# Two of the four slices of the experts' second product computed as split products

## The chip, the cores and the metric

One core of a Trainium2 chip runs the kernel. The metric is the device time of one execution in microseconds (us), as the median of several runs.

## The reference

One layer of a generator: a mixer (a recurrent part and an attention part, both on 1024 latent tokens behind 256 context tokens), and then a mixture of 32 experts, of which each token takes four. Only the experts matter here. For an expert with the tokens `xblk` gathered for it:

```python
u = xblk @ w1[e] + b1[e]                       # 1024 -> 2048
glu = jnp.minimum(u[:, 0::2], SWIGLU_LIMIT)
lin = jnp.clip(u[:, 1::2], -SWIGLU_LIMIT, SWIGLU_LIMIT)
return (glu * jax.nn.sigmoid(SWIGLU_ALPHA * glu) * (lin + 1.0)) @ w2[e] + b2[e]   # 1024 -> 1024
```

The rows are then scaled by the gates and added to the token stream, and a norm ends the layer. Everything is in float32.

## The kernel before

The mixer's instructions are put in order by a planner (class Weave), whose helper at line 954 issues them, so that they all carry that line. The last part of it routes the tokens, loads the first slices of the first expert and converts them (Route.loads, line 684, Route.conversions, line 698).

Then come 32 jobs, one for each expert, in a fixed order that lets sizes alternate (`TURN`, line 100). A job has N places for tokens: by `NS`, line 99, 13 jobs have 128, four 132, nine 136 to 156, three 160, and one each 168, 192 and 200. Experts.run (line 452) issues all instructions in the order written there, with no planner: each job has twelve steps, s = 0 to 11, one for each weight slice of 1 MB (128 x 2048 float32). Slices 0 to 7 belong to the first product, 8 to 11 to the second.

A slice of the first product is computed as a **split product**. ScalarE copies the slice into a rounded form, fp32r (hi, line 342, the instruction is at line 348); VectorE subtracts that from the slice and leaves the rest in bf16 (lo, line 351, at line 356). The tokens lie in both forms too, side by side (tokens, line 316: transposes at 326, ScalarE's copy at 328, VectorE's subtraction at 329). In products (line 371) 16 matmuls of the rounded weights go over both halves of the tokens, 2N columns (line 382), and 16 of the bf16 rests over the tokens' upper halves, N columns (line 386). sums (line 402) adds the two column halves of the result: ScalarE reads the second with the bias (407), VectorE adds the first (408) and clips (409, 410); gate (414) and hidden (417) follow.

A slice of the second product is computed **unsplit**, in plain float32 with N columns (line 393, 32 matmul instructions in the trace); ScalarE scales the result into yT (scaled, line 419, at 423). The first of them, s = 8, reads the hidden values of slices 6 and 7 last (`late`, line 390).

The tables `HI` and `LO` (lines 160, 161) say in which step which split slice, counted over the jobs, is converted:

```python
W1, W2 = 4, 4
HI = {0: 4, 1: 5, 2: 6, 3: 7, 5: 8, 7: 9, 8: 10, 9: 11}
LO = {s + 1: c for s, c in HI.items()}
```

So ScalarE converts four to two steps ahead of need, and VectorE one step after ScalarE. Converted slices have four places (ring "wc"), raw ones of the first product four (ring "w1") and of the second four (ring "w2"). lo asks SP for the load four split slices ahead (load1, line 362); run asks for the unsplit slices of the next job right after each unsplit product (load2, line 367), where SP waits until TensorE has read the place. SP's queue is in order.

Beside the slices, step 0 of a job computes the next job's slots (slots, line 283: matmuls at 292 on the one-hots, then eight small VectorE operations for each block of 128 tokens), step 1 starts its gather on GpSimd, step 8 transposes its tokens, and steps 8 to 11 make one-hots for the job after that, two in each step (onehots, line 275, at 281). Steps 1 to 4 transpose the job before's output rows (438, 439), and GpSimd scatters them (444). Results of the products go to two places of two PSUM banks in turn (ring "pe"); the slots' and transposes' go to four others.

Of the kernel before, what the change touches and what calls it, by code (L numbers as in the profile page):

```python
# [157 lines left out]

W1, W2 = 4, 4
HI = {0: 4, 1: 5, 2: 6, 3: 7, 5: 8, 7: 9, 8: 10, 9: 11}  # L160
LO = {s + 1: c for s, c in HI.items()}

# [17 lines left out]
class Experts:  # L180
# [23 lines left out]
    def place(self, sets):  # L204
# [16 lines left out]
        lo = HL  # L221
        for tag, n, width, dt in (("HH", 1, 8 * most, F32), ("u", 2, 2 * most, F32), ("sg", 2, most, F32)):
            self.ring(tag, cols(lo, n, width, dt))
            lo += n * width
        mid = lo
        assert lo + 2048 <= ROOM
        self.ring("yo", cols(sb + 3072, 3, D))
        self.ring("yT", cols(spare, 1, 8 * most))
        self.ring("wc", [(at(c, 2048, dt=F32R), at(c + 2048, 1024, dt=BF)) for c in (end, sa, sa + 3072, sb)])
        self.ring("w1", cols(sc, 3, 2048) + [at(low, 2048)])  # L230
        self.ring("w2", cols(end + 3072, 2, 2048) + [at(spare + 8 * most, 2048), at(mid, 2048)])
        lo = tt
# [99 lines left out]
    def load(self, J, s):  # L332
        nc = self.nc
        if s == 0:
            bi = self.t("bi", 24)
            nc.sync.dma_start(bi, self.a["bexp"][bass.ds(J["e"], 1)].rearrange("o p n -> p (o n)"))
            J["bi"] = bi
        w = self.t("w1" if s < 8 else "w2", 2048)
        nc.sync.dma_start(w, self.a["wexp"][bass.ds(J["e"], 1), s].rearrange("o p n -> p (o n)"))
        J["w", s] = w  # L340

    def hi(self, n):

        J, s = self.first(n)
        if J:
# [5 lines left out]
    def lo(self, n):  # L351

        J, s = self.first(n)
        if J:
# [3 lines left out]

    def first(self, n):
        return (self.jobs[n // 8], n % 8) if n < 8 * len(self.jobs) else (None, 0)  # L360

    def load1(self, n):
        J, s = self.first(n)
        if J:
            self.load(J, s)

    def load2(self, n):
        if n < 4 * len(self.jobs):
            self.load(self.jobs[n // 4], 8 + n % 4)

    def products(self, J, s):
# [3 lines left out]
        J["p", s] = p  # L375
        if s < 8:
            X = J["X"]
            xt = X.rearrange("p k s n -> p (k s n)").bitcast(BF).rearrange("p (k s n t) -> p k s n t", k=KT, s=2, t=2)
# [37 lines left out]
    def hidden(self, J, s):  # L416
        self.nc.vector.tensor_mul(J["H"][:, s], J.pop(("u", s))[:, 1], J.pop(("sg", s)))  # L417

    def scaled(self, J, s):
        nc, N, p = self.nc, J["N"], J.pop(("p", s))  # L420
        for q in range(2):
            c = 2 * s - 16 + q
            nc.scalar.activation(J["yT"][:, c], p[:, q, :N], AF.Identity, bias=J["b2"][:, 8 + c:9 + c],  # L423
                                 scale=self.gt2[:, c:c + 1])

# [26 lines left out]
    def run(self, fast=True, beside=None):  # L452
# [4 lines left out]
        for i in range(12 * len(jobs)):  # L457
# [4 lines left out]
            if s == 0:  # L462
                self.biases(J)
                J["H"] = self.t("HH", KT, J["N"])
                J["yT"] = self.t("yT", KT, J["N"])
# [9 lines left out]
            else:  # L475
                self.scaled(J, s)
                self.load2(4 * j + s - 4)
            if s in HI:
                self.hi(8 * j + HI[s])
            if s < 7:  # L480
                self.gate(J, s)
            if s in LO:
                self.lo(8 * j + LO[s])
            if s == 8 and nxt:
# [112 lines left out]
    def block(self, i):  # L597
# [19 lines left out]
        for s in range(4):  # L617
            self.hi(s)
            self.lo(s)
        self.run(False)  # L620
# [13 lines left out]
class Route:  # L634
# [49 lines left out]
    def loads(self):  # L684
        w, ex = self.w, self.ex
        yield self.placed
        yield self.rwkv.end
        for n, s in enumerate((0, 1, 2, 8, 9, 3, 10, 11)):
            if n == 3:
# [8 lines left out]
    def conversions(self):  # L698
        w, ex = self.w, self.ex
        for s in range(4):  # L700
# [3 lines left out]
            ex.hi(s)  # L704
            yield self.loaded[3]
            yield "dve"
# [2205 lines left out]
```

## Time and profile before

| | |
|---|---|
| median of 3 runs | 2736.94 us (2735.51 to 2742.81) |
| the profiled execution | 2734.6 us |
| its span, first to last instruction | 2732.8 us |
| TensorE busy | 2548.0 us, 93% of the span |
| VectorE, ScalarE busy | 1889.3 us (69%), 1461.1 us (53%) |
| first split product of the experts | 1267.86 us from the span's start |

In the rows PE is TensorE's matmuls, PEld its weight loads, DVE VectorE, ACT ScalarE, POOL GpSimd and SP the engine that issues most DMAs. Lengths of operations overlap on an engine; what an operation costs its engine is read from one start to the next. The idle time in square brackets is that ahead of the operation, with what ended it.

### The profile page before, as it was taken

Reading aid. Unit: us, or ns where it says so; the run is one execution under the profiler, and the core shown is the slowest. Engines: PE = TensorE matmul, PEld = TensorE weight load, DVE = VectorE, ACT = ScalarE, POOL = GpSimd, SP = SyncE. Lnnn points to the kernel's source line nnn. Section 1 sums busy time; section 2 is a strip of 40 time slices with the busy share of each in tenths; the row PEclk is TensorE's granted clock in tenths of the full one; section 3 lists DMA queues with packets and bytes.
Section 4 is the critical chain, followed back from the end, with each engine's and each line's share of the span. In section 5 each row is a group of like instructions: output and inputs, shape, how many; then the busy total and the mean of one; then the engine's idle time right before and its main releaser. Section 6 shows DMA issues by size and latency. Waiting matters only on the chain.

```text
span 2732.8 us, 58537 instructions
## 1 busy us (share of the span) xinstructions
PE 2548.0 (93%) x23428; PEld 2240.4 (82%) x23428; DVE 1889.3 (69%) x3925; ACT 1461.1 (53%) x2489; POOL 508.0 (19%) x455
## 2 busy tenths in 40 slices
PE   6999886989999997986999999999999999999996
PEld 3667664678677786665999999999999999999995
DVE  7745888867776638677676675766667676766765
ACT  6323333546544533234665665766656666666664
POOL 1112564411111136210011100110101010011101
PEclk8999987879999988997999999999999999999998
DMA  6741324253243145665887896988888988889884
GB/s 259 260 150 56 110 91 161 101 150 94 87 122 106 52 145 157 234 205 203 296 326 261 312 334 252 321 323 301 324 317 309 334 295 324 308 321 323 306 334 147
DMA packets 212183, 622.50 MB, mean 228 GB/s; under 512 B 49400, under 2 KB 127352, under 8 KB 160576
## 3 DMA queue, kind: packets, MB, share of 16 engines
q1 hardware_dynamic: 201008, 581.95, 59.1%
q0 software_dynamic: 10896, 36.74, 5.5%
q8 instruction: 186, 3.05, 0.4%
q14 instruction: 93, 0.76, 0.1%
HBM read 544.09 MB, written 74.53 MB: 226 GB/s over the span
## 4 chain that ended last, share of the span: by engine, by line
PE 72%; DVE 18%; DMA 3%; issue 3%; ACT 3%; POOL 1%; SPq 1%; DVEq 0%; ACTq 0%; POOLq 0%
PE banks L954 24%; PE banks L382 18%; PE banks L393 18%; DVE at L954 14%; PE banks L386 9%; ACT at L954 2%; DVE at L356 2%; PE banks L438 2%; PE banks L326 1%; POOL at L954 1%; DVE at L408 1%; SPq L954 1%; PE banks L292 0%; DVE at L409 0%; DMA at<-vh_d 0%
## 5 line engine op out<-in xcount | busy, mean ns | idle before, releaser
L954 PE MATMUL banks<-at,at 128*128 128x512 f32 (+10 forms) x3810 | 753.4, 355 | 54.4 <-POOL at L954 18.9
L954 PEld LDWEIGHTS banks<-at,at 128*128 128x128 f32 (+3 forms) x3290 | 451.4, 188 | 209.7 <-issue 82.3
L356 DVE TENSOR_TENSOR at<-at,at 128x2048 bf16<-128x2048 f32 x252 | 576.2, 2287 | 54.8 <-ACT at L348 53.9
L382 PE MATMUL banks<-at,at 128*128 128x256 f32 (+11 forms) x4096 | 601.8, 300 | 0.0
L382 PEld LDWEIGHTS banks<-at,at 128*128 128x128 f32 x4096 | 548.7, 190 | 1.2
L393 PE MATMUL banks<-at,at 128*128 128x128 f32 (+11 forms) x4096 | 521.5, 287 | 6.6 <-DVE at L417 6.0
L393 PEld LDWEIGHTS banks<-at,at 128*128 128x128 f32 x4096 | 505.0, 191 | 13.7 <-DVE at L417 12.9
L348 ACT ACTIVATE at<-at 128x2048 fp32r<-128x2048 f32 x252 | 481.5, 1911 | 0.0
L954 ACT ACTIVATE at<-banks 128x512 f32<-128x512 f32 (+6 forms) x475 | 239.6, 525 | 362.3 <-PE banks L954 339.5
L408 DVE TENSOR_TENSOR at<-banks,at 128x256 f32<-128x256 f32 (+11 forms) x256 | 115.6, 452 | 316.3 <-ACT at L407 304.3
L954 DVE TENSOR_TENSOR at<-at,at 128x1024 fp32r<-128x1024 f32 (+26 forms) x388 | 281.3, 736 | 57.0 <-ACT at L954 38.6
L407 ACT ACTIVATE at<-banks,at 128x128 f32<-128x128 f32 (+11 forms) x512 | 189.3, 380 | 226.1 <-PE banks L386 186.8
L386 PE MATMUL banks<-at,at 128*128 128x128 bf16 (+11 forms) x4096 | 306.0, 226 | 0.0
L954 ACT ACTIVATE at<-at 128x512 f32<-128x512 f32 (+10 forms) x259 | 175.9, 701 | 202.6 <-DVE at L954 108.3
L386 PEld LDWEIGHTS <-at 128*128 128x128 bf16 x4096 | 258.1, 96 | 17.6 <-issue 3.0
L954 PE MATMUL banks<-at 128*64 128x64 f32 (+4 forms) x4880 | 231.7, 232 | 36.8 <-DMA at<-w_d 18.6
L954 PEld LDWEIGHTS banks<-at 128*64 128x64 f32 (+3 forms) x4880 | 204.8, 143 | 68.7 <-issue 18.6
L954 POOL TENSOR_TENSOR at<-at,at 64x512 f32<-64x512 f32 (+5 forms) x130 | 185.9, 1439 | 308.0 <-DVE at L954 279.5
L423 ACT ACTIVATE at<-banks,at,modc 128x128 f32<-128x128 f32 (+11 forms) x256 | 116.9, 469 | 203.7 <-PE banks L393 203.5
L954 PE MATMUL banks<-kc,at 128*128 128x128 f32 (+4 forms) x1136 | 182.7, 291 | 44.5 <-ACT at L954 17.2
L312 POOL DMA_INDIRECT at<-h_d,at x49 | 47.5, 969 | 892.0 <-DVE at L294 364.1
L954 POOL TENSOR_TENSOR at<-at 128x512 f32<-128x512 f32 (+3 forms) x94 | 129.8, 1387 | 431.2 <-PE banks L954 132.3
(155 smaller groups left out, 2015.6 us busy)
## 6 DMA issues: line engine op xcount, KB each, us to landing
at<-in_wexp SPq DMA_DIRECT2D x384, 1024.0 KB
at<-in_mod_w SPq DMA_DIRECT2D x48, 512.0 KB
at<-w_d SPq DMA_DIRECT2D x48, 384.0 KB
w_d<-at SPq DMA_DIRECT2D x16, 1024.0 KB
at<-w_d SPq DMA_DIRECT2D x32, 512.0 KB
at<-in_w_in SPq DMA_DIRECT2D x18, 512.0 KB
x_d<-at SPq DMA_DIRECT2D x18, 512.0 KB
at<-in_x SPq DMA_DIRECT2D x16, 512.0 KB
```

Of the source, the lines that this page charges most:

```text
L312: nc.gpsimd.indirect_dma_start(out=xg[:R], out_offset=None, in_=self.d["h2"], in_offset=bass.IndirectOffsetOnAxis(ap=gi[:R, 0:1], axis=0))
L326: nc.tensor.transpose(p[:, k, :R], xg[:R, kk * 128:kk * 128 + 128], ident[:R, :R])
L348: self.nc.scalar.activation(wh, J["w", s], AF.Copy)
L356: self.nc.vector.tensor_sub(wl, J.pop(("w", s)), wh.bitcast(F32))
L382: nc.tensor.matmul(p[:, q, :2 * N], wh[:, k, q], X[:, k].rearrange("p s n -> p (s n)"), start=k == 0, stop=False, skip_group_check=True)
L386: nc.tensor.matmul(p[:, q, N:2 * N], wl[:, k, q], xt[:, k, 0, :, 1], start=False, stop=k == KT - 1, skip_group_check=True)
L393: nc.tensor.matmul(p[:, q, :N], w[:, k, q], J["H"][:, k], start=k == 0, stop=k == KT - 1, skip_group_check=True)
L407: nc.scalar.activation(u[:, q], p[:, q, N:2 * N], AF.Identity, bias=b)
L408: nc.vector.tensor_add(u, p[:, :, :N], u)
L423: nc.scalar.activation(J["yT"][:, c], p[:, q, :N], AF.Identity, bias=J["b2"][:, 8 + c:9 + c], scale=self.gt2[:, c:c + 1])
L438: nc.tensor.transpose(p[:R, k * 128:k * 128 + 128], J["yT"][:, 4 * j + k, b0:b0 + R], self.K("ident"))
L954: return f(*args, **kw)
```

## The change

Slices 10 and 11, the last two of the second product, become split products as well (`SPLIT`). So a job has ten split slices, which are counted and converted in the same rows of `HI` and `LO`, now with ten entries each; a conversion on VectorE that belongs to step 11's copy falls into step 0 of the next job (`LO[0] = 3`, thirteen slices on). The hidden values get two forms after step 7 (halves): ScalarE copies them into fp32r, VectorE subtracts, each in one instruction over all 8 x N columns. Slices 8 and 9 still read the plain values. In scaled the split slices take ScalarE's scaled reading of the second column half, and VectorE adds the first with the same scale (scalar_tensor_tensor). Raw slices of the split kind get five places, the unsplit ones two; the hidden values move to a place of their own. Before the first job seven slices are loaded by Route.loads instead of eight, and lo waits there for slice 4.

```diff
--- before.py
+++ after.py
@@ -156,9 +156,10 @@
     return o
 
 
-W1, W2 = 4, 4
-HI = {0: 4, 1: 5, 2: 6, 3: 7, 5: 8, 7: 9, 8: 10, 9: 11}
-LO = {s + 1: c for s, c in HI.items()}
+W1, W2 = 5, 2
+SPLIT = (0, 1, 2, 3, 4, 5, 6, 7, 10, 11)
+HI = {0: 4, 1: 5, 2: 6, 3: 7, 5: 8, 7: 9, 8: 10, 9: 11, 10: 12, 11: 13}
+LO = {0: 3, 1: 4, 2: 5, 3: 6, 4: 7, 6: 8, 8: 9, 9: 10, 10: 11, 11: 12}
 
 
 def inverse_root(e, y, x, t):
@@ -219,16 +220,16 @@
         self.tables, low = lo, HL - 2048
         assert lo + 400 <= low
         lo = HL
-        for tag, n, width, dt in (("HH", 1, 8 * most, F32), ("u", 2, 2 * most, F32), ("sg", 2, most, F32)):
+        for tag, n, width, dt in (("HH", 1, 16 * most, F32R), ("u", 2, 2 * most, F32), ("sg", 2, most, F32)):
             self.ring(tag, cols(lo, n, width, dt))
             lo += n * width
-        mid = lo
-        assert lo + 2048 <= ROOM
+        assert lo <= ROOM
         self.ring("yo", cols(sb + 3072, 3, D))
         self.ring("yT", cols(spare, 1, 8 * most))
         self.ring("wc", [(at(c, 2048, dt=F32R), at(c + 2048, 1024, dt=BF)) for c in (end, sa, sa + 3072, sb)])
-        self.ring("w1", cols(sc, 3, 2048) + [at(low, 2048)])
-        self.ring("w2", cols(end + 3072, 2, 2048) + [at(spare + 8 * most, 2048), at(mid, 2048)])
+        self.ring("w1", cols(sc, 3, 2048) + [at(low, 2048), at(spare + 8 * most, 2048)])
+        self.ring("w2", cols(end + 3072, 2, 2048))
+        self.ring("H", cols(spare + 8 * most + 2048, 1, 8 * most))
         lo = tt
 
         def one(n, dt=F32):
@@ -335,13 +336,13 @@
             bi = self.t("bi", 24)
             nc.sync.dma_start(bi, self.a["bexp"][bass.ds(J["e"], 1)].rearrange("o p n -> p (o n)"))
             J["bi"] = bi
-        w = self.t("w1" if s < 8 else "w2", 2048)
+        w = self.t("w1" if s in SPLIT else "w2", 2048)
         nc.sync.dma_start(w, self.a["wexp"][bass.ds(J["e"], 1), s].rearrange("o p n -> p (o n)"))
         J["w", s] = w
 
     def hi(self, n):
 
-        J, s = self.first(n)
+        J, s = self.split(n)
         if J:
             wh, wl = self.rings["wc"][0]
             self.rings["wc"].append(self.rings["wc"].pop(0))
@@ -350,31 +351,32 @@
 
     def lo(self, n):
 
-        J, s = self.first(n)
+        J, s = self.split(n)
         if J:
             wh, wl = J["c", s]
             self.nc.vector.tensor_sub(wl, J.pop(("w", s)), wh.bitcast(F32))
             self.load1(n + W1)
 
-    def first(self, n):
-        return (self.jobs[n // 8], n % 8) if n < 8 * len(self.jobs) else (None, 0)
+    def split(self, n):
+        j, i = divmod(n, len(SPLIT))
+        return (self.jobs[j] if j < len(self.jobs) else None), SPLIT[i]
 
     def load1(self, n):
-        J, s = self.first(n)
+        J, s = self.split(n)
         if J:
             self.load(J, s)
 
     def load2(self, n):
-        if n < 4 * len(self.jobs):
-            self.load(self.jobs[n // 4], 8 + n % 4)
+        if n < 2 * len(self.jobs):
+            self.load(self.jobs[n // 2], 8 + n % 2)
 
     def products(self, J, s):
         nc, N = self.nc, J["N"]
         p = self.rings["pe"][0]
         self.rings["pe"].reverse()
         J["p", s] = p
-        if s < 8:
-            X = J["X"]
+        if s in SPLIT:
+            X = J["X"] if s < 8 else J["HH"]
             xt = X.rearrange("p k s n -> p (k s n)").bitcast(BF).rearrange("p (k s n t) -> p k s n t", k=KT, s=2, t=2)
             wh, wl = (x.rearrange("p (k s c) -> p k s c", k=KT, s=2) for x in J.pop(("c", s)))
             for q in range(2):
@@ -416,12 +418,24 @@
     def hidden(self, J, s):
         self.nc.vector.tensor_mul(J["H"][:, s], J.pop(("u", s))[:, 1], J.pop(("sg", s)))
 
+    def halves(self, J):
+
+        HH = J["HH"] = self.t("HH", KT, 2, J["N"])
+        self.nc.scalar.activation(HH[:, :, 0], J["H"], AF.Copy)
+        self.nc.vector.tensor_sub(HH[:, :, 1], J["H"], HH[:, :, 0].bitcast(F32))
+
     def scaled(self, J, s):
         nc, N, p = self.nc, J["N"], J.pop(("p", s))
         for q in range(2):
             c = 2 * s - 16 + q
-            nc.scalar.activation(J["yT"][:, c], p[:, q, :N], AF.Identity, bias=J["b2"][:, 8 + c:9 + c],
-                                 scale=self.gt2[:, c:c + 1])
+            u = J["u2"] = self.t("u", 2, N) if s in SPLIT and q == 0 else J.get("u2")
+            nc.scalar.activation(u[:, q] if s in SPLIT else J["yT"][:, c], p[:, q, N:2 * N] if s in SPLIT else p[:, q, :N],
+                                 AF.Identity, bias=J["b2"][:, 8 + c:9 + c], scale=self.gt2[:, c:c + 1])
+        if s in SPLIT:
+            for q in range(2):
+                c = 2 * s - 16 + q
+                nc.vector.scalar_tensor_tensor(J["yT"][:, c], p[:, q, :N], self.gt2[:, c:c + 1], u[:, q],
+                                               op0=OP.mult, op1=OP.add)
 
     def rows(self, J, i):
 
@@ -461,7 +475,7 @@
             far = jobs[j + 2] if j + 2 < len(jobs) else None
             if s == 0:
                 self.biases(J)
-                J["H"] = self.t("HH", KT, J["N"])
+                J["H"] = self.t("H", KT, J["N"])
                 J["yT"] = self.t("yT", KT, J["N"])
             self.products(J, s)
             if s < 8:
@@ -474,13 +488,16 @@
                     self.hidden(J, s)
             else:
                 self.scaled(J, s)
-                self.load2(4 * j + s - 4)
+                if s not in SPLIT:
+                    self.load2(2 * j + s - 6)
             if s in HI:
-                self.hi(8 * j + HI[s])
+                self.hi(len(SPLIT) * j + HI[s])
             if s < 7:
                 self.gate(J, s)
-            if s in LO:
-                self.lo(8 * j + LO[s])
+            if s in LO and (i or not fast):
+                self.lo(len(SPLIT) * j + LO[s])
+            if s == 7:
+                self.halves(J)
             if s == 8 and nxt:
                 self.tokens(nxt)
             if j == 0 and nxt and s == 1:
@@ -616,7 +633,8 @@
         self.tokens(J)
         for s in range(4):
             self.hi(s)
-            self.lo(s)
+            if s < 3:
+                self.lo(s)
         self.run(False)
 
     def final(self, out):
@@ -685,7 +703,7 @@
         w, ex = self.w, self.ex
         yield self.placed
         yield self.rwkv.end
-        for n, s in enumerate((0, 1, 2, 8, 9, 3, 10, 11)):
+        for n, s in enumerate((0, 1, 2, 8, 9, 3, 4)):
             if n == 3:
                 yield self.outputs
             if n == 5:
@@ -702,7 +720,7 @@
             yield self.loaded[s]
             yield "act"
             ex.hi(s)
-            yield self.loaded[3]
+            yield self.loaded[4]
             yield "dve"
             ex.lo(s)
```

## Rows read from the trace of the kernel before

**Rows 1.** The page, part 4: the chain that ended last, by line
```profile
PE banks L954 24%; PE banks L382 18%; PE banks L393 18%; DVE at L954 14%; PE banks L386 9%; ACT at L954 2%; DVE at L356 2%; PE banks L438 2%; PE banks L326 1%; POOL at L954 1%; DVE at L408 1%; SPq L954 1%; PE banks L292 0%; DVE at L409 0%; DMA at<-vh_d 0%
```

**Rows 2.** Windows: span, busy PE PEld DVE ACT POOL, granted clock, DMA share, GB/s
```profile
1300.00:2680.00 1380.00, 1373.53 (x13104) 1344.16 (x13104) 946.92 (x2063) 886.16 (x1441) 142.19 (x97) 1.00 0.86 309
2222.37:2264.10 41.73, 41.37 (x435) 40.52 (x434) 30.41 (x71) 28.37 (x48) 7.31 (x4) 1.00 0.92 330
```

**Rows 3.** Timeline of TensorE, end of a 128-token job: start, us, line, form
```profile
2238.97 2.08 PE L382 MATMUL banks<-at,at 128*128 128x256 f32 x16
...
2247.55 1.55 PE L393 MATMUL banks<-at,at 128*128 128x128 f32 x12
2249.47 2.50 PE L393 MATMUL banks<-at,at 128*128 128x128 f32 x20 [0.36 <-DVE at L417]
...
2253.36 10.98 PE L393 MATMUL banks<-at,at 128*128 128x128 f32 x96
2264.10 2.43 PE L382 MATMUL banks<-at,at 128*128 128x296 f32 x16
```

**Rows 4.** Timeline of TensorE, the 148-token job behind it
```profile
2284.96 2.43 PE L382 MATMUL banks<-at,at 128*128 128x296 f32 x16
...
2288.26 2.42 PE L382 MATMUL banks<-at,at 128*128 128x296 f32 x16
...
2296.86 12.25 PE L393 MATMUL banks<-at,at 128*128 128x148 f32 x96
2308.85 2.16 PE L382 MATMUL banks<-at,at 128*128 128x256 f32 x16
```

**Rows 5.** Timeline of VectorE, one step of the 128-token job
```profile
2230.39 0.42 DVE L408 TENSOR_TENSOR at<-banks,at 128x256 f32<-128x256 f32 x1 [1.38 <-issue]
2230.85 0.23 DVE L409 TENSOR_SCALAR at<-at 128x128 f32<-128x128 f32 x1
2230.99 0.22 DVE L410 TENSOR_SCALAR at<-at 128x128 f32<-128x128 f32 x1
2231.13 0.28 DVE L417 TENSOR_TENSOR at<-at,at 128x128 f32<-128x128 f32 x1
2231.33 2.28 DVE L356 TENSOR_TENSOR at<-at,at 128x2048 bf16<-128x2048 f32 x1
2233.53 0.42 DVE L408 TENSOR_TENSOR at<-banks,at 128x256 f32<-128x256 f32 x1
```

**Rows 6.** Groups by line and form: busy us, mean ns, idle before
```profile
L348 ACT ACTIVATE at<-at 128x2048 fp32r<-128x2048 f32 x252 | 481.5, 1911 | 0.0
...
L954 ACT ACTIVATE at<-at 128x1024 fp32r<-128x1024 f32 x42 | 44.1, 1054 | 58.3 <-PE banks L954 31.3 <-DVE at L954 10.7 <-DMA at<-in_w_in 6.5
L954 DVE TENSOR_TENSOR at<-at,at 128x1024 fp32r<-128x1024 f32 x34 | 43.4, 1284 | 27.1 <-ACT at L954 17.1 <-PE banks L954 9.5 <-issue 0.2
...
L329 DVE TENSOR_TENSOR at<-banks,at 128x80 fp32r<-128x80 f32 x2 | 0.4, 231 | 0.0
...
L408 DVE TENSOR_TENSOR at<-banks,at 128x256 f32<-128x256 f32 x104 | 43.8, 421 | 118.5 <-ACT at L407 109.4 <-issue 8.9
...
L954 DVE SCALAR_TENSOR_TENSOR at<-banks,kc,at 128x512 f32<-128x512 f32 x10 | 7.4, 745 | 0.1
```

**Rows 7.** Timeline of VectorE around the turn of a job
```profile
2161.67 2.29 DVE L356 TENSOR_TENSOR at<-at,at 128x2048 bf16<-128x2048 f32 x1 [1.51 <-ACT at L348]
...
2212.96 0.42 DVE L281 TENSOR_SCALAR at<-at,at 128x148 bf16<-128x148 bf16 x2
...
2225.91 0.42 DVE L408 TENSOR_TENSOR at<-banks,at 128x256 f32<-128x256 f32 x1 [6.49 <-ACT at L407]
```

**Rows 8.** Waits of SP's queue: us in total, times, longest us
```profile
SPq L339 <- PE banks L393: 324.0, 124, 5.2
```

**Rows 9.** Windows, as in rows 2, before the first expert
```profile
1260.00:1265.00 5.00, 2.94 (x16) 2.20 (x14) 3.07 (x10) 3.28 (x5) 0.00 (x0) 0.50 0.02 5
```

**Rows 10.** Groups by line: the slot matmuls
```profile
L292 PE MATMUL banks<-at,at 128*128 128x8 bf16 x248 | 11.6, 167 | 3.1 <-DVE at L281 3.1
```

## The prediction

> **What bounds the kernel now.** I read the page's chain first: TensorE holds most of it, and behind the helper line of the mixer (24%) its pieces are lines 382 and 386 (split products, 18% and 9%) and 393 (unsplit ones, 18%) [rows 1]. Only the expert stage is changed, so I cut it out by windows: from 1300 to 2680 us TensorE is busy for 1373.5 of 1380 us at the granted clock 1.00, with VectorE at 947, ScalarE at 886 and the DMA share at 0.86 [rows 2]. So a job (one expert) costs what its matmuls cost. The only regular gap of TensorE there is at the first unsplit slice, 0.36 us in a job of 128 tokens [rows 3].
>
> **Term 1, matmuls removed: -46 us.** Prices are start-to-start times of whole slices. With 128 tokens three unsplit slices run from 2253.36 to 2264.10, 3.58 us each; three split ones from 2238.97 to 2247.55, 2.86 us each [rows 3]: 0.72 us saved per slice. With 148 tokens it is (2308.85 - 2296.86)/3 = 4.00 against 3.30, 0.70 saved [rows 4]. 26 of the 32 jobs have 128 to 156 tokens, six have 160 to 200 and hardly save less: 64 slices x 0.72 = 46 us. That is the ceiling: the rest of TensorE's work is the same.
>
> **Term 2, what VectorE must do more.** In a 128-token job of 41.73 us it is busy for 30.4 us [rows 2]. Added are two conversions (2.28 us long, but the next operation starts 2.20 us after: 2231.33 to 2233.53 [rows 5]), one subtraction of 128x1024 into fp32r (1.28 us), and four scalar_tensor_tensor of 128x128 out of PSUM [rows 6]. The last has no row of its own: above the 0.23 us of 128x80 and below the 0.42 us of 128x256, both plain sums out of PSUM; a scalar_tensor_tensor of 128x512 takes 0.75, on the line that these two make (0.23 + 432 x 0.0011 = 0.70) but for 0.05 [rows 6]. I take 0.33, midway. Together 4.4 + 1.3 + 1.3 = 7.0, so 37.4 us of work. The job's matmuls will need 41.73 - 2 x 0.72 = 40.3 us. That fits, but VectorE works in order, and I followed the order step by step:
>
> - Step 7: the subtraction of the second half stands behind ScalarE's copy (1.05 us [rows 6]), and that behind a conversion of 1.9 us. Before, VectorE already waited 1.51 us there for that conversion [rows 7]; now it waits about 2.5, then subtracts. Behind it stand the conversion of step 8, the subtractions of the next tokens and the one-hots. They move back by 2.2 us, and TensorE doesn't feel it there: slices 8 and 9 take the values as they were, and slice 10, the first reader of the halves, begins 9.4 us after slice 7's end (5.81 to the end of slice 8's transposes, 2247.55 to 2253.36, and 3.58 [rows 3]), the halves being ready after some 6.
> - Steps 8 to 11: 2.20 of conversion in each, 0.35 of one-hots in each (0.42 for two, end included [rows 7]), and 0.7 of scalar_tensor_tensor in steps 10 and 11. VectorE's idling ahead of each new job, 6.49 us here [rows 7], is used up.
> - The turn of the job. Slice 11 ends at time E. ScalarE's second read ends near E + 0.6, the second scalar_tensor_tensor near E + 0.9, the conversion that now stands in step 11 near E + 3.1, the two one-hots near E + 3.5. Ahead of them step 10 may still be at work, up to 0.3 more. TensorE has its slot matmuls (line 292), which read those one-hots, right behind slice 0: at E + 2.86 with 128 tokens, E + 3.30 with 148. **A new wait of TensorE on line 281**, 0.3 to 0.9 us in all but the largest jobs. I take 0.7 in 30 jobs: +21 us, bounds 9 and 27.
> - Steps 0 to 4: in step 0 a conversion is added ahead of the slots' small operations; then each step is 3.14 us (2230.39 to 2233.53 [rows 5]) against TensorE's 2.86 and a few transposes in a small job. Nothing is caught up until step 5, which has none. The hidden product of slice 6, for which the first unsplit slice waits, comes 0.1 to 0.8 later: 17 small jobs x 0.2 = +3 us, bounds 2 and 14.
>
> **What costs nothing.** ScalarE gets two conversions (1.91 each) and a copy: 28.4 + 4.9 of 41 us in a small job [rows 2, 6]; that is hidden under TensorE, and only the copy's place, priced above, matters. The loads are as many. 64 of the 128 that waited for TensorE's unsplit slices (324 us of SP's standing [rows 8]) now follow a conversion; chunk n + 5 is asked for when chunk n is converted, four or five steps ahead, 13 us or more, against 3.4 us for each slice in the stream (41 us over 12). Behind SP's wait stand only later loads and the small gate and bias reads. Before the first job lo() waits for one load more, but the DMA engines stand at 0.02 from 1260 to 1265, so it has landed [rows 9]. PSUM of slices 10 and 11 comes free 0.3 us later, still a slice ahead of need. The end gains two scalar_tensor_tensor ahead of the last transposes: +0.7 us.
>
> **The sum.** -46 + 21 + 3 + 1 = -21 us. The profiled execution took 2734.6 us (span 2732.8), 2.3 below the median of the three runs, so 2713.6 in its terms and about 2716 for a median of new runs.
>
> **A rule against the change.** The chain of [rows 5] shows that operations of VectorE overlap: the conversion is followed 0.08 us before its end, and five operations whose lengths add to 3.43 us take 3.14. The Trainium skill, VectorE: DVE Perf Modes, section "The DRAIN you can't avoid", says that the next operation does not start until the pipe is empty, and allows an earlier start only for one that is not held; the trace agrees with that exception. By the rule alone a small job would ask 37.4 + 4.2 (the overlaps of 71 operations) + 2.5 = 44.1 us of VectorE, 2.4 more than it takes now, and 17 of them would make the kernel some 40 us slower instead of 21 faster.
>
> **Rivals.** (a) VectorE is never late enough to hold TensorE: the idling at the turn was large, and TensorE waited 3.1 us in all for one-hots so far [rows 10]. Against it: the order above. It would give the ceiling, 2734.6 - 46, some 2690 as a median. Chance 0.12. (b) VectorE sets the pace. Place: the closed loop from its step 7 round to the next, with the wait of 2.5 us in it. In a small job it has 37.4 + 2.5 = 39.9 against 40.3. There each microsecond beyond what I priced is paid at some 25 of the 31 turns (the largest jobs have room): 0.85 us more a job and the gain is gone, 2 us more and it is -21 + 50 = 29 us slower, 2766. Operations that don't overlap would do it: 71 a job x 0.06 is 4 us. For it: the thin margin, four unmeasured operations, the waits between ScalarE and VectorE. Against: in steps 1 to 4 of today's small jobs VectorE already runs without a gap at 3.14 a step, and TensorE doesn't wait [rows 3, 5]. Chance slower 0.15, about even 0.17. (c) Loads hold the products: the small job's window moves 330 GB/s at a share of 0.92 [rows 2]; 1.7% less time asks for 0.94. A slice would have to take over 3.5 us in the stream. It would eat some 10 us: 2726. Chance 0.04.
>
> **How the numbers follow.** My case (TensorE still the bound, less one wait at each turn) has 0.52, with its own range, from the bounds of the terms (-46 + 9 + 2 + 1 = -34 and -46 + 27 + 14 + 1 = -4), from 2703 to 2733. About 0.3% (8 us) is what a measurement of this kernel can tell from no change. Faster: 0.52 + 0.12 + 0.04 = 0.68; same 0.17; slower 0.15. The range goes from the ceiling nearly reached, 2692 (waits of 2 us in all), to 2741, which takes in the even case of (b) and leaves out its slow one and a little of (a).
>
> **What would show it.** Right: line 393 with half its instructions, line 382 and 386 a quarter more; jobs of 128 tokens near 41 us; VectorE busy about 37 us of that; "DVE at L281" as the releaser of line 292's matmuls, some 20 us in 30 times; VectorE's gap ahead of a job gone; the wait on line 417 a little above 0.36 in a small job. Wrong: line 382 held by the conversions (line 356) or by the sums (line 408) in most small jobs, which is (b); line 356's conversions on ScalarE waiting for loads, which is (c); or TensorE at 99.5% as before, which is (a).

## The result, and the profile after

The changed kernel takes 2705.4 us (median of four runs, 2704.5 to 2719.4) against 2736.4 for the kernel before (2735.5 to 2742.8): a ratio of 0.9894, interval 0.9858 to 0.9929, 31 us less by the medians. The profiled execution took 2705.2 us, its span 2703.4. Forecast: 2716, range 2692 to 2741.

The same views as before, now with the line numbers of the changed kernel: split products at 384 and 388, unsplit ones at 395, slot matmuls at 293 on the one-hots of 282, VectorE's conversions at 357, sums at 409 (ScalarE) and 410, biases at 401 and 402, hidden values at 419, the halves at 424 and 425, scalar_tensor_tensor at 437. First the chain, which answers to [rows 1].

```profile
PE banks L972 24%; PE banks L384 15%; DVE at L972 15%; DVE at L357 9%; PE banks L395 8%; PE banks L388 7%; ACT at L972 2%; DVE at L410 2%; PE banks L327 1%; DVE at L411 1%; SPq L972 1%; ACT at L409 1%; ACT at L349 1%; DVE at L412 1%; PE banks L452 1%
```

The unsplit products fell from 18% to 8%. New in the chain is VectorE's conversion, 9% where it had 2%: VectorE now takes part in setting the pace of the experts. The windows (columns as in [rows 2]), the expert stage and one job of 128 tokens:

```profile
1300.00:2650.00 1350.00, 1333.56 (x13084) 1296.06 (x13084) 1153.89 (x2281) 1027.00 (x1532) 166.75 (x97) 1.00 0.90 315
2200.09:2241.18 41.09, 40.20 (x436) 39.12 (x434) 36.50 (x77) 32.74 (x52) 7.52 (x4) 1.00 0.93 324
```

That is the same job as in [rows 2]: 41.09 us instead of 41.73, VectorE busy for 36.5 instead of 30.4. TensorE's two gaps are in its timeline, the turn and the first unsplit slice, and, from the job behind it (148 tokens), the next turn:

```profile
2200.09 2.13 PE L384 MATMUL banks<-at,at 128*128 128x256 f32 x16
...
2203.00 0.29 PE L293 MATMUL banks<-at,at 128*128 128x8 bf16 x6
2203.67 0.63 PE L293 MATMUL banks<-at,at 128*128 128x8 bf16 x10 [0.38 <-DVE at L282]
2204.23 2.16 PE L384 MATMUL banks<-at,at 128*128 128x256 f32 x16
...
2227.97 2.50 PE L395 MATMUL banks<-at,at 128*128 128x128 f32 x20 [0.51 <-DVE at L419]
...
2244.51 0.66 PE L293 MATMUL banks<-at,at 128*128 128x8 bf16 x8
2245.02 2.42 PE L384 MATMUL banks<-at,at 128*128 128x296 f32 x16
```

Before the change the slot matmuls took 0.55 us from the first to the next slice in this job, now 1.23 (2203.00 to 2204.23): 0.68 lost, of which the row labels 0.38 as waiting. So I measure from start to start. I cut each of 29 jobs (the second to the thirtieth) at its first slot matmul, at slice 1, at the first unsplit slice, at the token transposes and at the unsplit slice behind them, and summed the differences from the kernel before:

| us over 29 jobs | slot matmuls | slices 1 to 7 | first unsplit slice | the rest | all |
|---|---|---|---|---|---|
| the change | +13.7 | +0.5 | +3.0 | -42.4 | -25.1 |

Each number is rounded by itself, and all come from one profiled execution of each kernel. The mixer's end also moved, 1267.86 to 1263.80 for the first split product. That is not the change's: in the changed kernel and its variants below the same mixer ends between 1252.7 and 1275.4, and the mixer of the kernel before at 1267.86 in one profile and at 1277.56 in another (e10). So the experiments are read by both: the 29 jobs from the timelines, and the ratio of the times.

Three groups by line, which answer to [rows 10] and, for the loads, to [rows 8], and the waits of SP's queue:

```profile
L293 PE MATMUL banks<-at,at 128*128 128x8 bf16 (+11 forms) x392 | 24.0, 169 | 10.1 <-DVE at L282 9.9
L395 PE MATMUL banks<-at,at 128*128 128x128 f32 (+11 forms) x2048 | 271.5, 289 | 11.8 <-DVE at L419 11.4
L349 ACT ACTIVATE at<-at 128x2048 fp32r<-128x2048 f32 x316 | 603.3, 1909 | 0.0
```
```profile
SPq L340 <- PE banks L395: 127.7, 62, 5.3
```

Half as many unsplit products, ScalarE's conversions never held up by a load, and SP's standing for TensorE down from 324 us in 124 times.

VectorE's order at a turn, where slice 11 ends at 2241.18:

```profile
2241.47 0.41 DVE L282 TENSOR_SCALAR at<-at,at 128x128 bf16<-128x128 bf16 x2
2241.79 0.61 DVE L437 SCALAR_TENSOR_TENSOR at<-banks,modc,at 128x128 f32<-128x128 f32 x2
2242.31 2.28 DVE L357 TENSOR_TENSOR at<-at,at 128x2048 bf16<-128x2048 f32 x1
2244.51 0.41 DVE L282 TENSOR_SCALAR at<-at,at 128x128 bf16<-128x128 bf16 x2
2244.84 0.17 DVE L401 TENSOR_SCALAR at<-at 128x8 f32<-128x8 f32 x1
...
2245.52 0.47 DVE L410 TENSOR_TENSOR at<-banks,at 128x296 f32<-128x296 f32 x1 [0.45 <-ACT at L409]
```

The 6.49 us of idling ahead of a job [rows 7] are gone but for 0.45. Two scalar_tensor_tensor take 0.52 us from start to start.

### The profile page after: what moved, and what is told of

It reads as the page before. It is cut to its first block, busy times and chain, and to the rows that moved or that the text cites. A ratio compares the mean times of both kernels' runs of the same rounds, so it can differ in the third digit from the quotient of the medians.

```text
span 2703.4 us, 58826 instructions
## 1 busy us (share of the span) xinstructions
PE 2510.6 (93%) x23428; PEld 2192.4 (81%) x23428; DVE 2108.5 (78%) x4149; ACT 1606.2 (59%) x2585; POOL 533.8 (20%) x455
## 4 chain that ended last, share of the span: by engine, by line
PE 57%; DVE 30%; ACT 5%; issue 3%; DMA 3%; SPq 1%; POOL 0%; DVEq 0%; ACTq 0%; POOLq 0%
PE banks L972 24%; PE banks L384 15%; DVE at L972 15%; DVE at L357 9%; PE banks L395 8%; PE banks L388 7%; ACT at L972 2%; DVE at L410 2%; PE banks L327 1%; DVE at L411 1%; SPq L972 1%; ACT at L409 1%; ACT at L349 1%; DVE at L412 1%; PE banks L452 1%
## 5 line engine op out<-in xcount | busy, mean ns | idle before, releaser
L384 PE MATMUL banks<-at,at 128*128 128x256 f32 (+11 forms) x5120 | 750.6, 299 | 1.1 <-DVE at L410 1.1
L357 DVE TENSOR_TENSOR at<-at,at 128x2048 bf16<-128x2048 f32 x316 | 722.1, 2285 | 0.0
L384 PEld LDWEIGHTS banks<-at,at 128*128 128x128 f32 x5120 | 684.8, 189 | 2.7 <-DVE at L410 1.4
L349 ACT ACTIVATE at<-at 128x2048 fp32r<-128x2048 f32 x316 | 603.3, 1909 | 0.0
L388 PE MATMUL banks<-at,at 128*128 128x128 bf16 (+11 forms) x5120 | 382.3, 226 | 0.0
L388 PEld LDWEIGHTS <-at 128*128 128x128 bf16 x5120 | 322.6, 96 | 21.9 <-issue 3.5
L395 PE MATMUL banks<-at,at 128*128 128x128 f32 (+11 forms) x2048 | 271.5, 289 | 11.8 <-DVE at L419 11.4
L409 ACT ACTIVATE at<-banks,at 128x128 f32<-128x128 f32 (+11 forms) x512 | 183.7, 376 | 156.3 <-PE banks L388 120.8
L395 PEld LDWEIGHTS banks<-at,at 128*128 128x128 f32 x2048 | 255.0, 191 | 18.8 <-DVE at L419 18.1
L972 PE MATMUL banks<-kc,at 128*128 128x128 f32 (+4 forms) x1136 | 179.7, 287 | 43.6 <-ACT at L972 17.7
L972 PEld LDWEIGHTS banks<-kc,at 128*128 128x128 f32 (+2 forms) x1136 | 139.7, 168 | 73.9 <-issue 24.9
L458 POOL DMA_INDIRECT x_d<-at,at x50 | 122.4, 2448 | 333.6 <-ACT at L409 132.1
```

What stands on the lines that cost most here:

```text
L349: self.nc.scalar.activation(wh, J["w", s], AF.Copy)
L357: self.nc.vector.tensor_sub(wl, J.pop(("w", s)), wh.bitcast(F32))
L384: nc.tensor.matmul(p[:, q, :2 * N], wh[:, k, q], X[:, k].rearrange("p s n -> p (s n)"), start=k == 0, stop=False, skip_group_check=True)
L388: nc.tensor.matmul(p[:, q, N:2 * N], wl[:, k, q], xt[:, k, 0, :, 1], start=False, stop=k == KT - 1, skip_group_check=True)
L395: nc.tensor.matmul(p[:, q, :N], w[:, k, q], J["H"][:, k], start=k == 0, stop=k == KT - 1, skip_group_check=True)
L409: nc.scalar.activation(u[:, q], p[:, q, N:2 * N], AF.Identity, bias=b)
```

## The experiments

All are edits of the changed kernel but e10, and each was timed together with the kernel before. Differences from the kernel before, us over 29 jobs, taken as above, one profile for each run; where an edit does not touch it, the rest repeats between -42.4 and -42.7:

| run | slot matmuls | slices 1 to 7 | first unsplit | the rest | all | ratio, interval |
|---|---|---|---|---|---|---|
| the change | +13.7 | +0.5 | +3.0 | -42.4 | -25.1 | 0.9894, 0.9858 to 0.9929 |
| e1 slots later | moved | | | | -28.4 | 0.9890, 0.9860 to 0.9919 |
| e2 one-hots early | 0.0 | +5.2 | +8.8 | -42.6 | -28.6 | 0.9884, 0.9858 to 0.9909 |
| e3a two conversions out | +13.7 | +0.6 | -3.5 | -42.6 | -31.7 | 0.9848, 0.9819 to 0.9877 |
| e3b the turn's one out | 0.0 | +0.6 | +2.3 | -42.7 | -39.8 | 0.9843, 0.9813 to 0.9873 |
| e4 biases early | +17.7 | +0.1 | +1.3 | -42.6 | -23.5 | 0.9902, 0.9865 to 0.9938 |
| e5 both early | 0.0 | +0.8 | +5.0 | -42.4 | -36.6 | 0.9851, 0.9817 to 0.9885 |
| e6 both early, late 2 | 0.0 | +1.5 | -13.6 | -42.5 | -54.7 | 0.9777, 0.9743 to 0.9811 |
| e7 one conversion twice | +56.0 | +23.0 | +2.3 | -40.5 | +40.8 | 1.0157, 1.0127 to 1.0187 |
| e8 late 2 alone | +21.2 | +0.7 | -13.7 | -42.5 | -34.3 | 0.9845, 0.9814 to 0.9877 |
| e9 halves' copy early | +13.7 | +0.6 | +3.0 | -42.5 | -25.1 | 0.9892, 0.9861 to 0.9923 |
| e10 before, late 2 | 0.0 | +0.1 | -13.8 | -0.1 | -13.8 | 0.9936, 0.9910 to 0.9962 |
| e11 e6, one conv. twice | +5.4 | +15.9 | -13.6 | -20.8 | -13.1 | 0.9912, 0.9883 to 0.9941 |

### Taking the turn's wait away: e1, e2

```diff
-            if nxt and s == (2 if j == 0 else 0):
+            if nxt and s == (2 if j == 0 else 1):
                 self.slots(nxt)
-            if nxt and s == (3 if j == 0 else 1):
+            if nxt and s == (3 if j == 0 else 2):
                 self.gather(nxt)
```

> Edit to the changed kernel: the next job's slots are computed in step 1 instead of 0, its gather starts in step 2. No work is added or left out. The structural theory: TensorE is still the bound, and what it lost at the turn (13.7 us more between slice 0 and slice 1, summed over the jobs) is only that the slot matmuls stand one slice too early for one-hots that end some 3.6 us after slice 11. One slice later they are 2.3 us early, so the whole wait goes and nothing takes its place: 2705.4 - 13 = 2692 us (2690 to 2695), and no idle time of TensorE on the one-hots. The rival (VectorE sets the pace of the small jobs, a wait that is removed comes back at another place): 2702 to 2707, with the wait now on the sums or the conversions.

e2 leaves the slots and moves the last two one-hots (the lines that take them from their old place are not shown):

```diff
+            if far and s == 11:
+                self.onehots(far, range(6, 8))
             if s in LO and (i or not fast):
                 self.lo(len(SPLIT) * j + LO[s])
```

> Edit to the changed kernel: in step 11 alone, VectorE's two one-hots come ahead of the conversion of 2.2 us instead of behind it. The same work in another order. The structural theory: the one-hots end some 1.4 us after slice 11's end instead of 3.6, ahead of slice 0's end at 2.9, so the wait at the turn goes as in the run with the later slots: 2692 us (2690 to 2696). The conversion ends 0.35 us later, which nothing notices. The rival (VectorE sets the pace): no gain, 2702 to 2707, since VectorE's work is the same.

Both missed. The wait on the one-hots is gone, but of the 13.7 us some 10 came back behind it, as the rival had it: ratios 0.989 and 0.988 as without the edit. The timelines of ScalarE and VectorE in e2, in a job whose slice 0 starts at 2203.69, show where it starts:

```profile
2207.57 0.37 ACT L409 ACTIVATE at<-banks,at 128x128 f32<-128x128 f32 x1 [0.87 <-DVE at L402]
```
```profile
2207.97 0.42 DVE L410 TENSOR_TENSOR at<-banks,at 128x256 f32<-128x256 f32 x1 [0.45 <-ACT at L409]
...
2227.35 0.42 DVE L410 TENSOR_TENSOR at<-banks,at 128x256 f32<-128x256 f32 x1 [0.61 <-ACT at L409]
```

ScalarE's second reading of slice 0 needs the job's biases, and these two small operations of VectorE stand behind the same conversion. So VectorE's sums of slice 0 begin 4.28 us after slice 11's end (in the changed kernel too, by its VectorE timeline at this turn: 2204.37 against 2200.09), and from there to the hidden values VectorE works at 3.14 us a step in a small job and doesn't catch up: in e2 its sums of slice 6 (2227.35) begin 1.16 us after TensorE starts slice 7, in the kernel before 0.63. The 0.61 us that it idles there is a wait for ScalarE, whose gates wait for VectorE's clips in their turn (137.8 us in e2's stage, in 115 times). In the changed kernel the wait on the one-hots ran beside that delay, and the same distance is 0.70; without that wait the delay shows, in e2's TensorE timeline and waits (us in total, times, longest; PEld is TensorE loading weights, which waits for places of PSUM that the sums free):

```profile
2231.56 2.50 PE L395 MATMUL banks<-at,at 128*128 128x128 f32 x20 [0.95 <-DVE at L419]
```
```profile
PE banks L395 <- DVE at L419: 14.8, 18, 1.0
PEld banks L384 <- DVE at L410: 3.8, 14, 1.1
```

In the changed kernel the first of these was 9.0 us in 18 times, the second 0.4 us, once.

### Less work, at two places: e3a, e3b

```diff
+            w = J.pop(("w", s))
+            if n < 10 or n % 10 not in (8, 9):
-            self.nc.vector.tensor_sub(wl, J.pop(("w", s)), wh.bitcast(F32))
+                self.nc.vector.tensor_sub(wl, w, wh.bitcast(F32))
```

e3b has (2,) in place of (8, 9).

> Edit to the changed kernel: VectorE's conversions of slices 10 and 11 (in steps 6 and 8) are left out, so these slices use an old rest; 4.4 us of VectorE's work a job less, none of it near the turn. The structural theory: the slots' wait stays (at least 11 of its 13.7 us), since slice 11's scalar_tensor_tensor waits for ScalarE there anyway; only the first unsplit slice's wait on the hidden values goes with the conversion of step 6, at most 11 us: 2694 to 2702. The rival (VectorE's work sets the pace): 4.4 us less in 25 small jobs takes all waits away, under 2685.

> Edit to the changed kernel: only VectorE's conversion of step 11 (the next job's slice 2) is left out, 2.2 us of its work a job, half of what the run without slices 10 and 11's conversions leaves out. The structural theory: it stands ahead of the last one-hots, so the slots' wait goes in full and the hidden values' wait stays: 2692 us (2690 to 2695). The rival (VectorE's work sets the pace): half the gain of the run that leaves out two conversions.

As the structural theory has it, by the jobs: twice the work left out far from the turn leaves the +13.7 and takes only the hidden values' wait (6.5 us); half of it, left out at the turn, gains 14.7. By place the work counts, not by amount. By the times alone the two can't be told apart. (In e3b hardly anything comes back at another place; the biases no longer stand behind a conversion there.)

### What stands behind that conversion: e4, e5

```diff
             if s == 0:
-                self.biases(J)
+                if j == 0:
+                    self.biases(J)
...
+            if s == 11 and nxt:
+                self.biases(nxt)
             if s in LO and (i or not fast):
```

e5 is e4 and e2 together.

> Edit to the changed kernel: only the next job's two small bias operations of VectorE (0.2 us) are moved, from behind step 11's conversion to ahead of it. The new theory (two things stand behind that conversion: the one-hots and the biases, and the biases hold ScalarE's second reading of slice 0 and so VectorE's chain of sums up to the hidden values; VectorE has no slack in that chain in a small job): the slots' wait stays at +13.7 us over 29 jobs, the chain starts 0.7 us earlier, and the wait of the first unsplit slice falls from +3.0 to about -3.5. The 29 jobs together go from -25 to -31 against the kernel before, the time from 2705 to 2699 us where the mixer takes as long. The rival (VectorE's total work sets the pace, its order does not matter): -25, unchanged.

> Edit to the changed kernel: in step 11 both the last two one-hots and the next job's biases come ahead of VectorE's conversion; the same work, another order. The new theory: the slots' wait goes (+13.7 to 0), and, as the chain of sums also starts 0.7 us earlier, it doesn't come back as it did when the one-hots alone were moved: slices 1 to 7 at +1, first unsplit slice at +2 to +3, 29 jobs together near -39.5 against the kernel before, as when the conversion itself was left out; about 2691 us. The rival (VectorE's total work sets the pace): near -28.6, as with the one-hots alone, 2702 us.

e5 came out as expected, 3 us short: -36.6, with the slots' wait gone and little in its place. e4 missed: the slots' wait grew by 4.0 us (the biases now hold the one-hots up, by about 0.15 us at 26 of the 29 turns), and the first unsplit slice gained 1.7 us instead of 6.5. VectorE's timeline in e4, steps 6 and 7 of a small job:

```profile
2223.12 0.42 DVE L410 TENSOR_TENSOR at<-banks,at 128x256 f32<-128x256 f32 x1 [1.25 <-ACT at L409]
...
2224.06 2.29 DVE L357 TENSOR_TENSOR at<-at,at 128x2048 bf16<-128x2048 f32 x1
2226.26 0.42 DVE L410 TENSOR_TENSOR at<-banks,at 128x256 f32<-128x256 f32 x1
...
2226.99 0.68 DVE L419 TENSOR_TENSOR at<-at,at 128x128 f32<-128x128 f32 x2
```

VectorE has caught up here (it waits 1.25 us for slice 6), and yet hidden comes late, because step 6's conversion and slice 7's sums stand ahead of it. This is a second floor of that wait, little below the first; TensorE still waited 0.44 us in this job. The kernel before stood on it too, 0.36 us [rows 3], and the changed kernel stands just above it: measured as in e2, its sums of slice 6 begin at 0.70 us, e4's at 0.63.

### The first unsplit slice: e8, e6, e10

```diff
-        late = 1 if s == 8 else 0
+        late = 2 if s == 8 else 0
```

> Edit to the changed kernel: only late = 2, the first unsplit slice reads the hidden values of slice 6 last too. The closed-loop theory (in a small job VectorE works without a gap from the halves to the turn, and what it does is not earlier by this): the wait of the first unsplit slice goes (from +3.0 to about -13 us over 29 jobs against the kernel before), but slice 11 ends earlier while the one-hots do not, so the slots' wait grows by half a microsecond in each small job: +13.7 to about +23; together near -32 against -25. The rival (each wait stands by itself and can be taken away by itself): the slots' wait stays at +13.7 and the whole 16 us are gained, -41.

> As the run with one-hots and biases ahead of the conversion; besides, the first unsplit slice reads the hidden values of slice 6 last as well (late = 2), so that TensorE waits for them some 1.3 us later. The new theory: the remaining wait there (some +2.5, in all about 9 us of idle over the kernel) goes: first unsplit slice at -4 to -6 against the kernel before, 29 jobs together -46 to -48, about 2684 us, and no wait on VectorE of over 2 us in all in the jobs. The rival (VectorE's closed loop of a small job is then the bound: 37.5 us of work and 2.5 of waiting against 40.2 us of TensorE): the wait comes back on the one-hots or on slice 10, and the 29 jobs stay above -43.

> The kernel before, with late = 2 alone. It had the same wait of the first unsplit slice, 6.0 us in 18 times by the releaser. VectorE has room at its turn (6.5 us idle ahead of a job), so nothing takes the wait's place: 29 jobs -10 to -14 against the kernel before, about 2725 us. Then 11 or so of the 30 us by which the best variant lies below the changed kernel are not the split's. The rival (its loop is closed too): no gain.

Alone (e8) the edit gains 16.7 us at the first unsplit slice and gives 7.5 back at the slots: -34.3, near the closed-loop theory's -32 and not the rival's -41. In the kernel before (e10) nothing is given back, as expected. With the turn in order (e6) all of it stays: TensorE has no gap left in a 128-token job (39.65 us, where the changed kernel has 41.09), and its waits for VectorE in the stage are down to 1.4 us:

```profile
2168.68:2208.33 39.65, 39.65 (x436) 38.91 (x433) 35.62 (x77) 32.72 (x52) 7.64 (x4) 1.00 0.94 335
```
```profile
PE banks L395 <- DVE at L419: 0.9, 1, 0.9
PE banks L384 <- DVE at L410: 0.5, 1, 0.5
```

e6 was 7 us better than expected: I had sized this wait by its labelled idle time, which shows only part of it. e6 takes 2674.7 us (2661.7 to 2691.5), 62.9 less than the kernel before timed with it, of which the jobs explain 54.7. It beats both kernels: 0.9777, where the change has 0.9894 and the kernel before with the same edit 0.9936. Against that last one the split is worth -54.7 + 13.8 = -40.9 us in 29 jobs.

### VectorE's load and its wait: e9, e7, e11

e9 moves ScalarE's copy for the halves ahead of its conversion in step 7 (the lines taken out of halves are not shown):

```diff
+            if s == 7:
+                HH = J["HH"] = self.t("HH", KT, 2, J["N"])
+                self.nc.scalar.activation(HH[:, :, 0], J["H"], AF.Copy)
             if s in HI:
                 self.hi(len(SPLIT) * j + HI[s])
```

> Edit to the changed kernel: in step 7 ScalarE's copy for the halves comes ahead of its conversion, so VectorE waits there some 0.6 us instead of 2.5. The theory so far: VectorE gains 1.9 us on the way to the turn, but the scalar_tensor_tensor of slice 11 waits there for ScalarE's reading of that slice, so the one-hots end as late as before: slots' wait +12 to +14, 29 jobs -24 to -27, no gain. The rival (b) of the prediction (VectorE's closed loop with its wait of 2.5 us sets the pace): 1.9 us less in some 17 small jobs, 10 us or more.

-25.1 as without it. But the edit did not take VectorE's waiting away. Its timeline in a small job, in the changed kernel and in e9 (lines 424 and 425, the subtraction of the halves):

```profile
2230.76 1.23 DVE L425 TENSOR_TENSOR at<-at,at 128x1024 fp32r<-128x1024 f32 x1 [2.45 <-ACT at L424]
```
```profile
2224.99 1.23 DVE L424 TENSOR_TENSOR at<-at,at 128x1024 fp32r<-128x1024 f32 x1 [1.12 <-ACT at L494]
2226.80 2.29 DVE L357 TENSOR_TENSOR at<-at,at 128x2048 bf16<-128x2048 f32 x1 [0.58 <-ACT at L349]
2229.78 1.58 DVE L330 TENSOR_TENSOR at<-banks,at 128x512 fp32r<-128x512 f32 x4 [0.69 <-ACT at L329]
```

One wait of 2.45 us became three of 2.39 in all, each for ScalarE. So e9 leaves the rival's loop untested. That the wait costs nothing at the turn is shown by e3a: with 4.4 us less work a job, VectorE only waits longer for ScalarE, and its first scalar_tensor_tensor of slice 11 still starts 0.61 us after that slice's end, 2238.97 against 2238.36 (in the changed kernel 2241.79 against 2241.18). VectorE's timeline in e3a:

```profile
2238.97 0.60 DVE L439 SCALAR_TENSOR_TENSOR at<-banks,modc,at 128x128 f32<-128x128 f32 x2
```

e7 does the conversion of step 9 twice (and the one of the first job, ahead of the 29 jobs):

```diff
+            w = J.pop(("w", s))
+            for _ in range(2 if n % 10 == 0 else 1):
-            self.nc.vector.tensor_sub(wl, J.pop(("w", s)), wh.bitcast(F32))
+                self.nc.vector.tensor_sub(wl, w, wh.bitcast(F32))
```

> Edit to the changed kernel: VectorE's conversion of step 9 is done twice, 2.2 us more of its work in each job, none of it on a slice that is wanted soon. The prediction's rival (b) in numbers: each microsecond more is paid at the turn of the small jobs, where VectorE has no idle time between the halves and the turn: 17 small jobs x 2.2 = 37, and the larger ones up to 1.2 each, +37 to +52 us, 2742 to 2757, all of it in TensorE's wait on the one-hots; slower than the kernel before. The rival theory (the wait at the turn is of fixed size, VectorE's idle time takes up the rest): under +10.

It is slower than the kernel before, 2782.8 us, and by more than either theory: 65.9 us over the change in 29 jobs. 42.3 of it is the slots' wait, within the bounds: 25 of the 29 turns pay, 1.7 us each, and the four behind the first job and the three largest don't. 22.5 is in slices 1 to 7, where nothing was added. TensorE's timeline and windows at one turn show what it is:

```profile
1752.39 2.32 PE L386 MATMUL banks<-at,at 128*128 128x280 f32 x16
1754.55 1.18 PE L390 MATMUL banks<-at,at 128*128 128x140 bf16 x16
1755.56 0.29 PE L293 MATMUL banks<-at,at 128*128 128x8 bf16 x6
1758.06 0.34 PE L293 MATMUL banks<-at,at 128*128 128x8 bf16 x2 [2.20 <-DVE at L282]
1758.26 3.68 PE L386 MATMUL banks<-at,at 128*128 128x280 f32 x16
1761.74 1.38 PE L390 MATMUL banks<-at,at 128*128 128x140 bf16 x16
```
```profile
1752.39:1755.56 3.17, 3.17 (x36) 1.00 0.93 336
1758.26:1761.74 3.48, 3.48 (x17) 0.57 0.91 353
```

After the wait of 2.20 us the granted clock is 0.57 over the next matmuls (1.2 GHz for most of them, 2.4 before): slice 1's first sixteen take 3.48 us from start to start (1758.26 to 1761.74) where slice 0's took 2.16 (1752.39 to 1754.55). It doesn't follow each such wait:

```profile
2303.04 0.34 PE L293 MATMUL banks<-at,at 128*128 128x8 bf16 x2 [2.03 <-DVE at L282]
```
```profile
2303.24:2306.59 3.35, 3.35 (x34) 1.00 0.94 352
```

By the granted clock of slices 1 to 7 it followed 14 of the 25 waits, and these 14 jobs hold 22.3 of the 22.5 us.

e11 puts the same dose (from the second job on) into e6:

> The best variant so far (one-hots and biases ahead of step 11's conversion, late = 2), with VectorE's conversion of step 9 done twice from the second job on, 2.2 us more of its work a job. The question is whether VectorE has room left there. The theory: in a job of 128 tokens it has none but what it waits for ScalarE (36.5 us of work and 3.1 of waiting in 39.65), so the 2.2 us are paid in full in some 17 small jobs and about 0.3 to 0.5 in the larger ones: 29 jobs from -54.7 to between -17 and -5 against the kernel before, more where TensorE's clock falls behind the waits. The rival (the order was all that was wrong, VectorE has room now): at most 1 us a small job, below -37.

-13.1, within the first theory's bounds: 41.6 us given back, 36.8 of them in the sixteen jobs of 128 and 132 tokens, 2.3 each, and 4.8 in the thirteen larger ones. The waits it left (us in total, times, longest; lines shifted by two):

```profile
PE banks L386 <- DVE at L439: 17.4, 19, 1.6
PE banks L386 <- DVE at L412: 7.1, 11, 0.9
```

TensorE now waits for places of PSUM that the sums and the scalar_tensor_tensor free late. So e6 has no room on VectorE in its small jobs: more work there is paid in full.

## Why the prediction was right

- **The bound and term 1.** TensorE sets the time of a job; a split slice saves what the start-to-start times said: 42.4 us over the 58 slices of 29 jobs is 0.73 each, forecast 0.72.
- **Term 2, the wait at the turn.** The mechanism, its place and its releaser are as forecast, but the term was mis-sized: +13.7 us over 29 jobs instead of +21. The step that failed is "I take 0.7 in 30 jobs". By its own working the one-hots end 3.5 us after slice 11 and slice 0 ends at 2.86 or at 3.30, so the wait is about 0.7 with 128 tokens and 0.2 with 148; I used the small job's figure for all sizes. VectorE's added work was close: 36.5 us in a small job, forecast 37.4 (a scalar_tensor_tensor takes 0.26 us, not 0.33). Measured: 0.68 in the job above, 0.30 with 148 tokens (0.51 from 2244.51 to 2245.02, 0.21 before), none in the three largest.
- **The hidden values.** +3.0, forecast +3. But the reason given, that steps 0 to 4 don't catch up, is only one of two floors of that wait (e4), and in the changed kernel the two lie within 0.1 us.
- **The halves** cost nothing at step 7, as said (e3a).
- **The end** was given +0.7 and cost more. Six of the 64 slices lie outside the 29 jobs and should have saved 4.3 us, but the stage outside them moved by only -0.2 us (span less mixer: 1464.9 to 1439.6, -25.3). So the two ends cost about 4 us. The last job has most of it, in TensorE's timeline at the first unsplit slice and in the windows of its last 15 matmuls (the changed kernel's, then that of the kernel before):

```profile
2655.01 6.07 PE L395 MATMUL banks<-at,at 128*128 128x128 f32 x52 [2.32 <-DVE at L419]
2675.03:2680.34 5.31, 5.31 (x15) 3.91 (x15) 3.16 (x7) 2.90 (x8) 2.06 (x2) 0.68 0.00 0
```
```profile
2705.32:2709.14 3.82, 3.81 (x15) 2.66 (x15) 2.48 (x4) 2.55 (x8) 1.83 (x2) 1.00 0.00 0
```

  Step 6 of the last job had no conversion before, since no job follows, and no wait was labelled there; now slice 10's stands in it, ahead of the end's one-hots and of slice 7's sums, and the hidden values come 2.3 us late. The last matmuls took 1.5 us longer, at a granted clock of 0.68 instead of 1.00, behind a wait for ScalarE of 2.37 us (2.13 in the kernel before).
- **The sum.** -21 forecast, -25.3 in the stage: the turn's wait was put some 7 us too high and the ends some 3 too low, so the errors partly cancel. The other 4 us by which the span fell are the mixer's, which differs by more than that between profiles.
- **Rival (a)**, VectorE never late, didn't hold for the change. Its ceiling exists: e6 and e3b take the wait away, e6 by order alone.
- **Rival (b)**, VectorE sets the pace, did not decide the sign but is the nearest to what I missed. Its count was right, 25 of the 29 turns paid in e7, at 1.7 of 2.2 us each; but the clock's fall, which it left out, added half as much again, so that 65.9 us came where its price gives 55. And in small jobs VectorE does set the pace from slice 0's sums to the hidden values; e1 and e2 failed because I had taken the turn's wait for the only thing that VectorE holds up. The biases behind the conversion were in the code, in the list of what is queued there, and I left them out.
- **Rival (c)**, loads: no conversion on ScalarE waits for one, and 335 GB/s at 0.94 go through in e6's job.
- **The rule on operations of VectorE that don't overlap** would have made the kernel 40 us slower; the conversion at 2242.31 above is followed 2.20 us after its start though it is 2.28 long, as in the kernel before.

## What to carry to other kernels

A wait can lie beside another one of the same cause: list everything that stands behind the late instruction, each with its reader, and move all of it, or the second shows as soon as the first is gone. In a loop that two engines share, work counts by its place: 4.4 us left out far from the turn gave less than 2.2 at it, and reordering the turn gave nearly as much as leaving its work out (36.6 us against 39.8), for nothing. Size a wait job by job with its own slice length, and measure it from start to start, for labelled idle time shows only part of it.

## What the runs showed of the hardware that was not expected

Waits of TensorE at the turn can cost more than their length: behind a wait of 2.20 us in e7 the granted clock was 0.57 over the next 3.48 us, and some 1.3 us were lost there; over 29 jobs slices 1 to 7 grew by 22.5 us. It is no matter of length alone in these runs: the stretch of the slot matmuls had grown by 1.7 to 2.9 us where the clock fell in e7, and by 1.2 to 2.7 where it did not. In the changed kernel, which loses 0.8 us at most at a turn, and in e11, with waits of up to 1.6 us, it did not fall in the 29 jobs. Which of two waits of the same length it follows stays open.
